# A decoder trunk on one core: who makes the second weight tile's high part in the front, and how many filler matmuls stand there

## The chip, the core and the metric

The kernel runs on one core of a Trainium2 chip. The metric is the device time of one execution in microseconds (us). Five engines run their own instruction queues side by side: TensorE (PE; PEld is its weight load), VectorE (DVE), ScalarE (ACT), GpSimd (POOL) and SyncE (SP), which mostly issues DMAs. Before the change the time is 1191.01 us, the median of three runs (1190.72 to 1191.04).

## What is computed

The reference is a small decoder with two layers, 512 tokens and 1024 columns: layer 0 mixes tokens with forgetting attention, layer 1 with a gated short convolution, and each has a squared-ReLU MLP and a gated embedding. Only the very first product matters here, the value projection of the attention:

```python
def rmsnorm(x, g):
    xf = x.astype(jnp.float32)
    y = xf * lax.rsqrt(jnp.mean(xf * xf, axis=-1, keepdims=True) + RMS_EPS)
    return (y * g.astype(jnp.float32)).astype(x.dtype)
...
hn = rmsnorm(x, g[0])
proj = hn @ w_in
v = proj[..., 2 * D:3 * D]
f_logit = (proj[..., 3 * D:] + b_f)
```

## The kernel before

**High and low parts.** All products are made with float32 data that is split into a high part (rounded to the matmul's input format) and a low part (what the rounding left). A product is three matmuls: high x high, low x high and high x low. For a weight tile `raw` the high part `wh` is a scaled copy, and the low part `wl` is `raw` times the scale minus `wh`. The scale is the gain `g` of the norm, one number per partition.

**The value projection** works on `x` as it came, transposed by the host (`xT`), with the gain folded into the weights; the token's norm is applied to the result. Its columns go in three chunks (`V_CHUNKS`); the first has 272 columns, 256 of values and 16 forget-gate logits. `part(c, ps, t, n, fill)` makes the twelve matmuls of chunk c, token block t (of 4) and half n of the contraction (four weight tiles): four with `wh` and `xh`, four with `wh` and `xl`, four with `wl` and `xh`, line 690. The tile of `x` is the stationary operand, the weight tile is streamed, 272 columns at a time.

**The order around the change** is written out by hand (a manual schedule for all engines). SyncE and ScalarE issue the first DMAs (from line 2320): the first block of `xT`, the weight tiles 0 to 3 and then the next blocks. Weight tile 0 (`in_wg`) carries the gains of three norms in 24 more columns; tile 1 comes over SyncE, tile 2 over ScalarE, tile 3 over SyncE. TensorE first runs seven matmuls on a tile of ones (`work(7)`, line 2335), which nobody reads; I call these fillers. VectorE casts the first block of `xT` to its high part (line 838) and copies the gains to `first_g` (line 841); GpSimd makes that block's low part `xl` (line 842). Then `prepare(4)` gives, tile by tile, ScalarE the high part and VectorE the low part (lines 481 and 483). The first ScalarE copy takes its scale from the raw tile, since `first_g` isn't there yet; the other three take it from `first_g`. The first call of `part` gets `fill = (1, 1, 1)`: behind each of its first three matmuls TensorE runs one 512-column filler. After it, the other three token blocks follow, each with its own split of `xT` (ScalarE high, VectorE low, lines 472 and 473), and so on without fillers.

**Beyond the front** the kernel goes through attention, the MLPs, the convolution and the gated embeddings, with the order of work from a planner; the change touches none of it.

Of the kernel before, what the change touches and what calls it, by code (L numbers as in the profile page):

```python
# [8 lines left out]
F32 = mybir.dt.float32  # L9
F32R = mybir.dt.float32r  # L10
AF = mybir.ActivationFunctionType
ALU = mybir.AluOpType
# [3 lines left out]
P = 128  # L16
D = 1024
S = 512
# [6 lines left out]
NEG = -1e30  # L25
PUT_OFF = 46000
LAG = 2
AHEAD = 2
PAGES = 70
RAWS = 14  # L30
LEAD = 1
V_CHUNKS = ((768, 272), (0, 512), (512, 256))
# [182 lines left out]
def trunk(ctx: ExitStack, tc, x, xT, pT, g, wg, wv, wqk, bf, wo, wci, wcq, cw, wco, wup, wdn, wpp, wpg, out):  # L215
    nc = tc.nc
# [10 lines left out]
    def page(name, dtype=F32):  # L227
        return pages.tile([P, S], dtype, tag="pg", name=name)
# [12 lines left out]
    warm = page("warm", F32R)  # L241
# [4 lines left out]
    first_g = consts.tile([P, 3 * KT], F32, tag="first_g", name="first_g")  # L246
# [4 lines left out]
    loads, order, where, ready, fetched, begun = [], [], {}, {}, [], [0]  # L251
# [61 lines left out]
            ],  # L313
        )

    def widest(key):

        return V_CHUNKS[key[1]][1] if key == ("v", 0, 0) else S

    def fetch(upto, engines=(nc.sync,)):  # L320
        while len(fetched) < min(upto, len(loads)):
            n = len(fetched)
# [5 lines left out]
    def banked(key):  # L328

        return key[0] in ("up", "dn") and key[2] // (1 + (key[0] == "up")) in BANKED  # L330
# [25 lines left out]
    def prepare(upto, lows=None):  # L356
        while begun[0] < min(upto, len(order)):
            n = begun[0]
            begun[0] += 1
            key, at = order[n]  # L360
            for of in (key[:3], key[:2]):
                if of in recipes and banked(key):
                    if of not in fetched_of:
                        at_of = recipes[of][0]
                        fetch(max(at_of.values()) + 1)
                        fetched_of[of] = {u: fetched[m] for u, m in at_of.items()}
                    if isinstance(at, tuple):
                        sum_in_bank(of, key[len(of):])
                elif of in recipes:
                    derive(of)  # L370
            hi, lo = page(f"wh{n}", F32R), page(f"wl{n}", F32R)
            if isinstance(at, tuple):
                raw, w = derived[key] if banked(key) else derived.pop(key), S
                eng = nc.gpsimd if (key[0] == "dn" and key[2] > 0) or key[-1] in ON_POOL else nc.vector
                if banked(key):
                    eng = nc.vector
            else:
                fetch(at + 1)
                raw, eng, w = fetched[at], lows or nc.vector, min(loads[at].shape[-1], widest(key))
                if banked(key) and low_on_pool(key):  # L380
                    eng = nc.gpsimd
                fetched[at] = None
            if key[0] in ("v", "qk"):
                split_gained(hi, lo, raw, w, key[2], eng, key[0] == "qk" or key[1] == 2,
                             raw[:, w : w + 1] if key == ("v", 0, 0) else None)
            else:
                split(hi[:, :w], lo[:, :w], raw[:, :w], eng)
            ready[key] = Pair(hi[:, :w], lo[:, :w])

    def wide(*key, soon=SOON):  # L390

# [80 lines left out]
        nc.scalar.copy(hi, src)  # L472
        return eng.tensor_tensor(out=lo, in0=src, in1=hi.bitcast(F32), op=ALU.subtract)

    def split_gained(hi, lo, src, w, at, eng, paired, first=None):

        parts = [(slice(0, w), at)]
        if paired:
            parts = [(slice(256 * i, 256 * i + 256), 2 * at + i) for i in range(2)]
        for c, k in parts:  # L480
            nc.scalar.mul(hi[:, c], src[:, c], first_g[:, k : k + 1] if first is None else first)
        for c, k in parts:
            eng.scalar_tensor_tensor(
                out=lo[:, c], in0=src[:, c], scalar=first_g[:, k : k + 1],
                in1=hi[:, c].bitcast(F32), op0=ALU.mult, op1=ALU.subtract,
            )
# [139 lines left out]
    def attention(hT, raw_x, b_f, warm, work, by_hand):  # L626
# [59 lines left out]
        def part(c, ps, t, n, fill=()):  # L686

            for p, of in ("hi", "hi"), ("lo", "hi"), ("hi", "lo"):
                for k in range(4 * n, 4 * n + 4):
                    nc.tensor.matmul(  # L690
                        ps[:, : V_CHUNKS[c][1]], getattr(of_x(k, t), p),
                        getattr(ready["v", c, k], of),
                        start=k == 0 and p == of, stop=k == KT - 1 and of == "lo",
                    )
                    if p == of and k < len(fill):
                        work(fill[k])

        def values(t):

# [127 lines left out]
        with tc.manual_schedule(engines={E.PE, E.DVE, E.Activation, E.Pool, E.SP}):  # L827
            work(7)
            banks_v = {(0, t): bank(f"v0_{t}") for t in range(NB)}

            def halves(c, *at):
                for t, n in at:
                    if (c, t) not in banks_v:
                        banks_v[c, t] = bank(f"v{c}_{t}")
                    part(c, banks_v[c, t], t, n, (1, 1, 1) if c == t == n == 0 else ())

            first = turned[0, 0] = Pair(*(page(f"x{s}0_0", F32R) for s in "hl"))
            nc.vector.tensor_copy(first.hi[:, :S], raw_x[0][0][:, :S])
            w = V_CHUNKS[0][1]
            gains = fetched[0][:, w : w + 3 * KT]  # L840
            nc.vector.tensor_copy(first_g, gains)
            nc.gpsimd.tensor_tensor(
                out=first.lo[:, :S], in0=raw_x[0][0][:, :S], in1=first.hi[:, :S].bitcast(F32),
                op=ALU.subtract,
            )
            prepare(4)
            halves(0, (0, 0))
            for t in range(1, NB):
                split_x(t, 0)
                halves(0, (t, 0))  # L850
                if t == 2:
                    prepare(6)
            prepare(KT)
            fetch(2 * KT)
            nc.sync.dma_start(b_f, bf[0:1, :].partition_broadcast(P))
            first_x = [load_x("xc", t) for t in range(NB)]
            fetch(RAWS + KT)
            for t in range(NB):
                split_x(t, 1)
                halves(0, (t, 1))  # L860
            tri, ones = page("tri", F32R), page("ones")
            nc.gpsimd.memset(ones[:, :S], 1.0)
            nc.gpsimd.affine_select(
                out=ones[:, :S], in_=ones[:, :S], compare_op=ALU.is_ge, fill=0.0, base=0,
                pattern=[[1, S]], channel_multiplier=-1,
            )
            nc.vector.tensor_copy(tri[:, :S], ones[:, :S])
            prepare(KT + 4)
            halves(1, (0, 0), (1, 0))
            prepare(2 * KT)  # L870
            fetch(RAWS + 2 * KT)
            halves(1, (0, 1), (1, 1))
            for t in range(NB):
                inverse(t)
            halves(1, (2, 0))
            r_rows = rows()
            halves(1, (2, 1), (3, 0), (3, 1))
            for two in ((0, 1), (2, 3)):
                for t in two:
                    logits(t, banks_v[0, t])  # L880
                for t in two:
                    keep_values(0, t, banks_v[0, t])
                prepare(2 * KT + 4)
            steps = logs()
            first_half = normed_x(0, r_rows)
            next(first_half)
            next(steps)
            next(first_half)
            keep_values(1, 0, banks_v[1, 0])
            next(steps)  # L890
            next(first_half)
            keep_values(1, 1, banks_v[1, 1])
            next(steps)
            fetch(RAWS + 2 * KT + 4)
            for _ in first_half:
                pass
            for t in range(1):
                values(t)
            sums_of_logs(tri)
            bias(0)  # L900
            bias(1)
            keep_values(1, 2, banks_v[1, 2])
            prepare(2 * KT + 6)
            for _ in normed_x(1, r_rows):
                pass
            prepare(2 * KT + 8)
            keep_values(1, 3, banks_v[1, 3])
            for t in range(1, NB):
                values(t)
            for n, _ in enumerate(project(0, 0)):  # L910
                if n == KT - 1:
                    prepare(2 * KT + 12)
        def heads_planned():
# [255 lines left out]
            n_sc, done = 4 * H, 8  # L1169
            for c in range(-8, n_sc + LAG):  # L1170
                share = 2 * (c + 9) if c < n_sc - 16 else (
# [1158 lines left out]
    b_f = consts.tile([P, H], F32, tag="bf", name="b_f")  # L2330
    warm_p = bank("warm_p")

    def work(n):
        for _ in range(n):
            nc.tensor.matmul(warm_p, warm[:, :P], warm[:, :S], start=True, stop=True)

    kept = dram.tile([2, NB, 2, P, S], F32, tag="kept", name="kept")
    hT = turned_x
# [119 lines left out]
```

## Time and profile before

| what | us |
|---|---|
| median of three runs | 1191.01 |
| the profiled execution | 1191.42 |
| its span, first to last instruction | 1189.5 |
| TensorE busy | 1180.9 |
| VectorE busy | 1023.0 |
| ScalarE busy | 871.2 |
| GpSimd busy | 610.4 |

The profile is of one execution. "Busy" counts an engine's instructions; a busy TensorE is not TensorE at its peak, since matmuls are pipelined and their durations overlap. The chain is the work that ended last, followed back step by step to what released it. In a timeline a row has the start, the duration, the engine, the line, the operation, output and inputs and the count of merged instructions; a number in square brackets is idle time of the engine before the row, and what ended it. In the rows on DMA issues the last number is the time from issue to landing. The 0.01 us of the views is their rounding, for landings 0.1.

### The profile page before, as it was taken

How to read it: one execution, taken by the hardware profiler on the slowest of the kernel's cores; microseconds unless marked ns; L12 is line 12 of the kernel's file. 1: busy time of each engine (PE TensorE's matmuls, PEld its weight loads, DVE VectorE, ACT ScalarE, POOL GpSimd, SP SyncE). 2: the span in 40 equal slices, each digit the busy share in tenths (PEclk: the TensorE clock that was granted, in tenths of full speed). 3: DMA queues.
4: the chain of work that ended last, by engine and by line, in shares of the span. 5: the costliest groups of instructions: out<-in, count | busy, mean ns of one | idle time of the engine just before them, and what ended most of it. 6: DMA issues, size and time to landing. Idle time of an engine off the chain costs nothing.

```text
span 1189.5 us, 21339 instructions
## 1 busy us (share of the span) xinstructions
PE 1180.9 (99%) x7220; PEld 1059.2 (89%) x7220; DVE 1023.0 (86%) x1789; ACT 871.2 (73%) x1867; POOL 610.4 (51%) x616
## 2 busy tenths in 40 slices
PE   9999999999999999999999999999999999999997
PEld 8888888898899889989889999989889998999886
DVE  7878988589989999988869999858999999998973
ACT  7688888469887888777756766447978878887751
POOL 3035567148557755776313653025775577559410
PEclk9999999999999999999999999999999999999999
DMA  9376754514233324356413233532332333236401
GB/s 340 112 218 167 210 183 116 195 63 119 80 113 115 112 74 136 106 171 201 143 36 99 67 104 115 188 123 63 116 107 84 121 116 115 84 112 205 142 18 53
DMA packets 86606, 149.96 MB, mean 126 GB/s; under 512 B 10144, under 2 KB 17872, under 8 KB 86496
## 3 DMA queue, kind: packets, MB, share of 16 engines
q1 hardware_dynamic: 85920, 148.04, 40.4%
q8 instruction: 57, 0.93, 0.3%
q10 hardware_dynamic: 576, 0.55, 0.1%
q14 instruction: 53, 0.43, 0.1%
HBM read 137.99 MB, written 6.37 MB: 121 GB/s over the span
## 4 chain that ended last, share of the span: by engine, by line
PE 92%; DVE 5%; issue 1%; ACT 1%; DMA 0%; POOL 0%; POOLq 0%; DVEq 0%
PE dn L465 8%; PE dn L464 8%; PE dn L466 8%; PE v L690 3%; PE qk L464 3%; PE qk L466 2%; PE qk L465 2%; PE pg L466 2%; PE pg L464 2%; PE pg L465 2%; PE ps_o L1104 2%; PE up L465 2%; PE up L466 2%; PE up L464 2%; PE pT L1076 1%; PE up_1c L466 1%
## 5 line engine op out<-in xcount | busy, mean ns | idle before, releaser
L1325 ACT CAST wh<-raw 128x512 fp32r<-128x512 f32 x261 | 157.1, 626 | 0.0
L1225 DVE TENSOR_TENSOR acc<-dn,acc 128x512 f32<-128x512 f32 x184 | 118.6, 679 | 6.4 <-PE dn L466 5.8
L1225 POOL TENSOR_TENSOR wl<-raw,wh 128x512 fp32r<-128x512 f32 x86 | 116.6, 1359 | 6.6 <-ACT wh L1325 6.3
L1225 POOL TENSOR_TENSOR s<-m,d 128x256 f32<-128x256 f32 x22 | 16.5, 752 | 156.7 <-ACT m L1745 137.4
L1325 ACT CAST wh<-dn_T 128x512 fp32r<-128x512 f32 x112 | 65.2, 588 | 28.7 <-DVE dn_T L1225 28.4
L1225 DVE TENSOR_TENSOR wl<-up_S,wb 128x512 fp32r<-128x512 f32 x104 | 68.2, 677 | 13.6 <-ACT wb L1329 11.9
L1325 ACT CAST wh<-up_S 128x512 fp32r<-128x512 f32 x104 | 65.5, 630 | 16.6 <-POOL up_S L1225 15.5
L1225 POOL TENSOR_TENSOR up_S<-raw,raw 128x512 f32<-128x512 f32 x52 | 77.0, 1489 | 0.0
L1225 DVE TENSOR_TENSOR wl<-dn_T,wh 128x512 fp32r<-128x512 f32 x112 | 74.6, 680 | 2.7 <-ACT wh L1325 2.7
L1329 ACT CAST wb<-up_S 128x512 fp32r<-128x512 f32 x104 | 62.1, 598 | 9.0 <-DVE acc L1225 4.5
L1225 DVE TENSOR_TENSOR wl<-raw,wb 128x512 fp32r<-128x512 f32 x100 | 65.7, 676 | 2.5 <-ACT wb L1329 2.5
L1225 DVE TENSOR_TENSOR wl<-raw,wh 128x512 fp32r<-128x512 f32 x75 | 60.9, 829 | 4.2 <-ACT wh L1325 4.1
L1329 ACT CAST wb<-raw 128x512 fp32r<-128x512 f32 x100 | 58.9, 596 | 0.0
L464 PE MATMUL qk<-hTh,wh 128*128 128x512 f32 x128 | 51.0, 398 | 0.0
L464 PE MATMUL pg<-wh,hTh 128*128 128x512 f32 x128 | 50.5, 395 | 0.0
L466 PE MATMUL qk<-hTl,wh 128*128 128x512 f32 x128 | 50.2, 392 | 0.0
L465 PE MATMUL qk<-hTh,wl 128*128 128x512 f32 x128 | 50.2, 392 | 0.0
L466 PE MATMUL pg<-wl,hTh 128*128 128x512 f32 x128 | 49.9, 390 | 0.0
L465 PE MATMUL pg<-wh,hTl 128*128 128x512 f32 x128 | 49.8, 389 | 0.0
L1063 POOL TENSOR_SCALAR prl<-prl,rs 128x512 f32<-128x512 f32 x16 | 25.9, 1617 | 44.0 <-DVE rs L1056 44.0
L465 PE MATMUL dn<-wh,S1l 128*128 128x512 f32 x112 | 43.9, 392 | 0.0
L466 PE MATMUL dn<-wl,S1h 128*128 128x512 f32 x112 | 43.7, 390 | 0.0
(846 smaller groups left out, 4956.1 us busy)
## 6 DMA issues: line engine op xcount, KB each, us to landing
raw<-in_wup SPq DMA_DIRECT2D x128, 256.0 KB, 2.9
raw<-in_wdn SPq DMA_DIRECT2D x128, 256.0 KB, 2.7
raw<-in_wcq SPq DMA_DIRECT2D x36, 256.0 KB, 2.8
raw<-in_wqk SPq DMA_DIRECT2D x32, 256.0 KB, 5.2
raw<-in_wpg SPq DMA_DIRECT2D x32, 256.0 KB, 2.8
g<-in_g SPq DMA_DIRECT2D x18, 256.0 KB, 5.5
raw<-in_wo SPq DMA_DIRECT2D x16, 256.0 KB, 4.4
prl<-neg_c SPq DMA_DIRECT2D x16, 256.0 KB, 4.8
```

The costliest lines, as they stand in the source:

```text
L464: nc.tensor.matmul(ps, a.hi, b.hi, start=start, stop=False)
L465: nc.tensor.matmul(ps, a.lo, b.hi, start=False, stop=False)
L466: nc.tensor.matmul(ps, a.hi, b.lo, start=False, stop=stop)
L690: nc.tensor.matmul(ps[:, : V_CHUNKS[c][1]], getattr(of_x(k, t), p), getattr(ready["v", c, k], of), start=k == 0 and p == of, stop=k == KT ...
L1063: nc.gpsimd.tensor_scalar(out=pr, in0=pr, scalar1=stats_of[h][1][:, u : u + 1], scalar2=None, op0=ALU.mult)
L1076: nc.tensor.transpose(ps[0][:, b * P : (b + 1) * P], probs[h][b][:, j * P : (j + 1) * P], ident)
L1104: nc.tensor.matmul(mixed[h][:, j * P :], v, u[:, j * P : S], start=j == 0 and not (stop or last.get(("u", h))), stop=stop)
L1225: eng.tensor_tensor(out=out, in0=x, in1=y, op=op)
L1325: nc.scalar.copy(ready[key].hi[:, both], src())
L1329: nc.scalar.copy(aside[0].bitcast(F32R), src())
```

## The change

Three things change, all in the first microseconds:

- A new function `prepare_first` replaces `prepare(4)`. It makes the four high parts first, with the second tile's on VectorE (a tensor_scalar multiplication) and the others on ScalarE, and puts the four low parts behind all four highs. All of them take their scale from the gains in raw tile 0.
- The copy of the gains to `first_g` moves behind the second tile's high part on VectorE. Later tiles still read `first_g`.
- The fillers in the first `part` become `FILLS = ((0,), (1, 256), (1,))`: none behind the first matmul, one of 256 columns behind the second, one of 512 behind the third.

```diff
+FILLS = ((0,), (1, 256), (1,))
+FIRST_ON_VECTOR = (1,)
...
+    def prepare_first(gains):
+
+        lows = []
+        for n in range(4):
+            key, at = order[n]
+            begun[0] += 1
+            raw, w, scale = fetched[at], V_CHUNKS[0][1], gains[:, n : n + 1]
+            hi, lo = page(f"wh{n}", F32R), page(f"wl{n}", F32R)
+            if n in FIRST_ON_VECTOR:
+                nc.vector.tensor_scalar(
+                    out=hi[:, :w], in0=raw[:, :w], scalar1=scale, scalar2=None, op0=ALU.mult
+                )
+            else:
+                nc.scalar.mul(hi[:, :w], raw[:, :w], scale)
+            fetched[at] = None
+            ready[key] = Pair(hi[:, :w], lo[:, :w])
+            lows.append((raw, scale, hi, lo, w))
+        nc.vector.tensor_copy(first_g, gains)
+        for raw, scale, hi, lo, w in lows:
+            nc.vector.scalar_tensor_tensor(
+                out=lo[:, :w], in0=raw[:, :w], scalar=scale, in1=hi[:, :w].bitcast(F32),
+                op0=ALU.mult, op1=ALU.subtract,
+            )
...
-                    if p == of and k < len(fill):
-                        work(fill[k])
+                    if fill:
+                        work(*fill.pop(0))
...
-                    part(c, banks_v[c, t], t, n, (1, 1, 1) if c == t == n == 0 else ())
+                    part(c, banks_v[c, t], t, n, fills if c == t == n == 0 else [])
...
-            nc.vector.tensor_copy(first_g, gains)
...
-            prepare(4)
+            prepare_first(gains)
...
-    def work(n):
+    def work(n, columns=S):
         for _ in range(n):
-            nc.tensor.matmul(warm_p, warm[:, :P], warm[:, :S], start=True, stop=True)
+            nc.tensor.matmul(
+                warm_p[:, :columns], warm[:, :P], warm[:, :columns], start=True, stop=True
+            )
```

The rest of the diff takes out what `split_gained` and `prepare` needed for the special case of the first tile.

The first rows of TensorE before, from the seven fillers to the first matmul of the low part of `x` (`wh0` to `wh3` are the high parts of the four weight tiles, `xh0_0` and `xl0_0` the high and low part of the first block of `x`):

```order
L2335 MATMUL warm_p_140<-warm_78 128x512 x7
L690 MATMUL v0_0_156<-wh0_165,xh0_0_160 128x272
L2335 MATMUL warm_p_140<-warm_78 128x512
L690 MATMUL v0_0_156<-wh1_169,xh0_0_160 128x272
L2335 MATMUL warm_p_140<-warm_78 128x512
L690 MATMUL v0_0_156<-wh2_173,xh0_0_160 128x272
L2335 MATMUL warm_p_140<-warm_78 128x512
L690 MATMUL v0_0_156<-wh3_177,xh0_0_160 128x272
L690 MATMUL v0_0_156<-wh0_165,xl0_0_161 128x272
```

The same place of TensorE now:

```order
L2357 MATMUL warm_p_140<-warm_78 128x512 x7
L711 MATMUL v0_0_156<-wh0_164,xh0_0_160 128x272
L711 MATMUL v0_0_156<-wh1_167,xh0_0_160 128x272
L2357 MATMUL warm_p_140<-warm_78 128x256
L711 MATMUL v0_0_156<-wh2_170,xh0_0_160 128x272
L2357 MATMUL warm_p_140<-warm_78 128x512
L711 MATMUL v0_0_156<-wh3_173,xh0_0_160 128x272
L711 MATMUL v0_0_156<-wh0_164,xl0_0_161 128x272
```

The filler between the first two matmuls is gone, and the next one is half as wide.

The first rows of VectorE before (`wl` are the low parts of the weight tiles, `xl1_0` the low part of the second block of `x`):

```order
L838 CAST xh0_0_160<-xT0_0_93 128x512
L841 COPY first_g_86<-raw0_102 128x24
L483 SCALAR_TENSOR_TENSOR wl0_166<-raw0_102,first_g_86,wh0_165 128x272
L483 SCALAR_TENSOR_TENSOR wl1_170<-raw1_104,first_g_86,wh1_169 128x272
L483 SCALAR_TENSOR_TENSOR wl2_174<-raw2_106,first_g_86,wh2_173 128x272
L483 SCALAR_TENSOR_TENSOR wl3_178<-raw3_108,first_g_86,wh3_177 128x272
L473 TENSOR_TENSOR xl1_0_197<-xT1_0_95,xh1_0_196 128x512
```

The same place of VectorE now:

```order
L861 CAST xh0_0_160<-xT0_0_93 128x512
L396 TENSOR_SCALAR wh1_167<-raw1_104,raw0_102 128x272
L404 COPY first_g_86<-raw0_102 128x24
L406 SCALAR_TENSOR_TENSOR wl0_165<-raw0_102,wh0_164 128x272
L406 SCALAR_TENSOR_TENSOR wl1_168<-raw1_104,raw0_102,wh1_167 128x272
L406 SCALAR_TENSOR_TENSOR wl2_171<-raw2_106,raw0_102,wh2_170 128x272
L406 SCALAR_TENSOR_TENSOR wl3_174<-raw3_108,raw0_102,wh3_173 128x272
L494 TENSOR_TENSOR xl1_0_196<-xT1_0_95,xh1_0_195 128x512
```

`wh1` has come in behind the cast, ahead of the copy of the gains; the low parts keep their order, and ScalarE loses `wh1` between `wh0` and `wh2`. GpSimd's and SyncE's rows stay in place, and from the second block of `x` on TensorE's, VectorE's and ScalarE's do too.

More of the change, by code (lines that the diff above doesn't have):

```diff
@@ L314, in plan_sevens @@
         )
-    def widest(key):
-        return V_CHUNKS[key[1]][1] if key == ("v", 0, 0) else S
     def fetch(upto, engines=(nc.sync,)):
@@ L378, in prepare @@
                 fetch(at + 1)
-                raw, eng, w = fetched[at], lows or nc.vector, min(loads[at].shape[-1], widest(key))
+                raw, eng, w = fetched[at], lows or nc.vector, loads[at].shape[-1]
                 if banked(key) and low_on_pool(key):
@@ L383, in prepare @@
             if key[0] in ("v", "qk"):
-                split_gained(hi, lo, raw, w, key[2], eng, key[0] == "qk" or key[1] == 2,
-                             raw[:, w : w + 1] if key == ("v", 0, 0) else None)
+                split_gained(hi, lo, raw, w, key[2], eng, key[0] == "qk" or key[1] == 2)
             else:
@@ L473, in split, with split_gained @@
         return eng.tensor_tensor(out=lo, in0=src, in1=hi.bitcast(F32), op=ALU.subtract)
-    def split_gained(hi, lo, src, w, at, eng, paired, first=None):
+    def split_gained(hi, lo, src, w, at, eng, paired):
         parts = [(slice(0, w), at)]
@@ L480, in split_gained @@
         for c, k in parts:
-            nc.scalar.mul(hi[:, c], src[:, c], first_g[:, k : k + 1] if first is None else first)
+            nc.scalar.mul(hi[:, c], src[:, c], first_g[:, k : k + 1])
         for c, k in parts:
@@ L829, in attention @@
             banks_v = {(0, t): bank(f"v0_{t}") for t in range(NB)}
+            fills = list(FILLS)
             def halves(c, *at):
```

## The prediction

> **What bounds the kernel now.** I read the page's busy time, its chain and TensorE's (PE's) own waits first, to see what a change in the first microseconds can be worth at all.
>
> ```profile
> PE 1180.9 (99%) x7220; PEld 1059.2 (89%) x7220; DVE 1023.0 (86%) x1789; ACT 871.2 (73%) x1867; POOL 610.4 (51%) x616
> PE 92%; DVE 5%; issue 1%; ACT 1%; DMA 0%; POOL 0%; POOLq 0%; DVEq 0%
> PE warm_p L2335 <- POOL warm L242: 1.4, 1, 1.4
> PE up_0a L465 <- DVE wl L1225: 0.3, 2, 0.2
> ```
>
> TensorE is busy for 99% of the span, the chain that ended last runs on it for 92%, and its waits add up to 1.7 us. No DMA has a share of the chain. So a matmul that starts x us earlier in the front brings the end x us nearer, unless something near the front is late. The chain in order of time shows the front.
>
> ```profile
> 0.78 3.42 DMA raw<-in_wg
> ...
> 4.23 0.53 ACT wh L481
> ...
> 4.80 0.60 PE v L690
> ...
> 7.13 23.05 PE v L690 x142
> ```
>
> The first weight tile lands, ScalarE (ACT) makes its high part `wh0`, TensorE starts at 4.80 and never stops again here. The timeline of TensorE in this stretch:
>
> ```profile
> 1.36 3.35 PE L2335 MATMUL warm_p<-warm 128*128 128x512 f32 x7 [1.36 <-POOL warm L242]
> 4.80 0.60 PE L690 MATMUL v<-wh,xh 128*128 128x272 f32 x1
> 5.19 0.63 PE L2335 MATMUL warm_p<-warm 128*128 128x512 f32 x1
> 5.62 0.43 PE L690 MATMUL v<-wh,xh 128*128 128x272 f32 x1
> 5.85 0.63 PE L2335 MATMUL warm_p<-warm 128*128 128x512 f32 x1
> 6.27 0.43 PE L690 MATMUL v<-wh,xh 128*128 128x272 f32 x1
> 6.50 0.63 PE L2335 MATMUL warm_p<-warm 128*128 128x512 f32 x1
> 6.93 0.43 PE L690 MATMUL v<-wh,xh 128*128 128x272 f32 x1
> 7.15 0.84 PE L690 MATMUL v<-wh,xl 128*128 128x272 f32 x4
> 7.38 0.61 PE L690 MATMUL v<-wh,xl 128*128 128x272 f32 x3
> 7.83 0.67 PE L690 MATMUL v<-wl,xh 128*128 128x272 f32 x4
> 8.34 0.66 PE L690 MATMUL v<-wh,xh 128*128 128x272 f32 x4
> ```
>
> Durations overlap, so I go by starts. Up to 7.38 a 272-column matmul takes 0.227 us from start to start (7.15 to 7.38) and a 512-column filler 0.43 (5.19 to 5.62, and likewise the other two). From 7.83 on, four 272-column matmuls take 0.51, or 0.127 each. TensorE's clock nearly doubles between 7.38 and 7.83. In the row of 7.38 the last of three starts at 7.71 (7.38 + 0.61, less the 0.66 - 3 x 0.127 = 0.28 that one takes), so the short spacing begins at about 7.59, and I put the change at 7.55.
>
> **The change part by part.** *TensorE.* The filler after the first matmul goes and the next one is halved: 0.43 + 0.21 = 0.64 us at the slow clock. The new starts, if every operand is there: first matmul up to 5.19, second 5.19, 256-column filler 5.42, third 5.63, filler 5.86, fourth 6.29, the low-part matmuls from 6.51 instead of 7.15. What counts is how far TensorE is when its clock rises. If that stays at 7.55, it is 0.64 / 0.227 = 2.8 matmuls ahead there, and each of these would have taken 0.127 at the fast clock: **a gain of 0.36 us**. If the clock rose 0.64 earlier too, the whole 0.64 would be gained; I take the fixed time, because nothing removed lets TensorE be busy any earlier.
>
> *Operands.* ScalarE, VectorE (DVE) and GpSimd (POOL) in the same stretch, with the issues and landings of the weight tiles:
>
> ```profile
> 4.23 0.52 ACT L481 ACTIVATE wh<-raw 128x272 fp32r<-128x272 f32 x1 [1.03 <-DMA raw<-in_wg]
> 4.66 0.52 ACT L481 ACTIVATE wh<-raw,first_g 128x272 fp32r<-128x272 f32 x1
> 5.57 0.53 ACT L481 ACTIVATE wh<-raw,first_g 128x272 fp32r<-128x272 f32 x1
> 4.03 0.43 DVE L838 CAST xh<-xT 128x512 fp32r<-128x512 f32 x1 [4.03 <-DMA xT<-in_xT]
> 4.37 0.17 DVE L841 COPY first_g<-raw 128x24 f32<-128x24 f32 x1
> 4.54 1.27 POOL L842 TENSOR_TENSOR xl<-xT,xh 128x512 fp32r<-128x512 f32 x1 [2.71 <-DVE first_g L841]
> 4.78 2.92 DVE L483 SCALAR_TENSOR_TENSOR wl<-raw,first_g,wh 128x272 fp32r<-128x272 f32 x4 [0.24 <-ACT wh L481]
> 4.78 1.33 DVE L483 SCALAR_TENSOR_TENSOR wl<-raw,first_g,wh 128x272 fp32r<-128x272 f32 x1 [0.24 <-ACT wh L481]
> 6.03 0.49 DVE L483 SCALAR_TENSOR_TENSOR wl<-raw,first_g,wh 128x272 fp32r<-128x272 f32 x1
> 1.23 0.89 SPq L326 DMA_DIRECT2D raw<-in_wv  x2
> raw<-in_wv ACTq DMA_DIRECT2D x1, 136.0 KB, 3.6
> raw<-in_wv SPq DMA_DIRECT2D x1, 136.0 KB, 3.3
> raw<-in_wv SPq DMA_DIRECT2D x1, 136.0 KB, 3.9
> ```
>
> `wh2` and `wh3` stay on ScalarE. Tile 2, issued beside tile 1 at 1.23, lands at 1.23 + 3.6 = 4.83, so `wh2` is done at 4.83 + 0.52 = 5.35, wanted at 5.63. Tile 3, SyncE's second issue at about 1.7, lands at 5.6; its copy already starts at 5.57 now and ends at 6.10 as before, wanted at 6.29. Taking `wh1` off ScalarE thus gains nothing for `wh3`, and the filler that stays covers that landing. Reading the scales from the raw tile is worth nothing alone: the second ScalarE copy ran 0.43 behind the first, by its own pace.
>
> `wh1` is the one that decides. Its tile lands at 1.23 + 3.3 = 4.53, known to 0.05 because the view rounds. The new VectorE operation is not in this trace; its nearest rows are the same operation on another tile:
>
> ```profile
> L671 DVE TENSOR_SCALAR neg_c<-c_T 16x384 f32<-16x384 f32 x1 | 0.4, 401 | 0.0
> L671 DVE TENSOR_SCALAR neg_c<-c_T 16x256 f32<-16x256 f32 x1 | 0.3, 334 | 0.0
> ```
>
> 272 columns lie 16 above 256: 334 + 16 x 67/128 = 342 ns. Tile 0 landed at 4.20 and was read at 4.23, so the new operation starts 0.03 behind its tile, at 4.56; undisturbed, `wh1` is there at 4.90, 0.29 before TensorE wants it at 5.19. Behind it in VectorE's queue wait the copy of the scales (only the fifth tile's copy, some 3 us later, needs it), the four low parts and the first `xl`. No DMA issue and no GpSimd or SyncE instruction changes place. The low parts are hardly moved: the first now takes 1.33 where an undisturbed one takes 0.49, because it sits behind GpSimd's operation (4.54 to 5.81), and so it would again. They end at 4.78 + 2.92 = 7.70; TensorE would want the fourth at about 7.9. That cover is 0.2 us. Should VectorE's new operation hold GpSimd up instead by some 0.3, the low parts end near 8.0 and TensorE waits about 0.2, which leaves 0.16 of the gain. Between 0.16 and 0.36 I take 0.3, nearer to the unhindered end, because only the last of four low parts would be late.
>
> **The weak point** is that GpSimd's operation starts at 4.54, the same moment at which tile 1 lands. Two pairs elsewhere show what such a meeting does:
>
> ```profile
> 874.00 1.83 POOL L1225 TENSOR_TENSOR up_S<-raw,raw 128x512 f32<-128x512 f32 x1
> 874.01 0.68 DVE L1225 TENSOR_TENSOR S1l<-s,S1h 128x512 fp32r<-128x512 f32 x1
> 969.18 1.29 POOL L1225 TENSOR_TENSOR wl<-raw,wh 128x512 fp32r<-128x512 f32 x1
> 969.23 1.79 DVE L1225 TENSOR_TENSOR dn_T<-raw,raw 128x512 f32<-128x512 f32 x1
> ```
>
> 0.01 us behind GpSimd, VectorE went first and GpSimd took 1.83; 0.05 behind, VectorE took 1.79 where it needs 0.68. Starting between 4.51 and 4.61, the new operation would come 0.03 before to 0.07 behind GpSimd's. But each of these VectorE operations reads two tensors; the new one reads one tensor and a column of scales, and no row here shows such an operation held up. GpSimd's row also names the copy of the scales as what it waited for, though it reads only the cast's output: if that is right, GpSimd now starts behind the new operation and the meeting is off. So I bound `wh1` by 4.90 and by the end of GpSimd's operation, 5.81, plus about 0.17 (272 columns at 67 ns per 128 are 0.14, and some start-up): 5.98. I forecast the first end: on the rows, only two-tensor operations are held.
>
> [...]
>
> **Rivals.** *VectorE is held and the clock rises late (slower).* `wh1` at 5.98 leaves TensorE without work from 5.19 to 6.03, for the filler that stood there is gone. Second matmul 6.03, filler 6.26, third 6.47, filler 6.70, fourth 7.13, low parts from 7.35: 0.20 behind now, or 0.20 / 0.227 x 0.127 = 0.11 at the end. The price is the clock. Before, it rose 7.55 - 4.80 = 2.75 after the unbroken run began, and 7.55 - 1.36 = 6.2 after the first filler. If the hole of 0.84 starts this anew at 6.03, it rises between 8.8 and 12.2, and TensorE runs slow for 1.25 to 4.65 us longer: 5.5 to 20.5 matmuls at 0.100 more, 0.55 to 2.05, with the 0.11 a loss of 0.66 to 2.16. The middle, 1.4, gives 1192.4. It decides once `wh1` comes so late that the hole outweighs what counted as busy before. For it: the race is close, and the pause before (4.71 to 4.80) was small beside this hole. [...]
>
> *VectorE is held, the clock rises on time.* Then only the 0.11 is lost: 1191.1. For it: fillers from 1.36 may count for the clock whatever follows.
>
> *The gain is eaten later, or the change does nothing.* Low parts, `xl1` or a transfer come late and take the rest: 1191.0. Against it: with 0.2 us of cover for the low parts, more would have to go late than the rows show.
>
> **How the numbers follow.** The profiled execution took 1191.42, 1.92 more than its span of 1189.5; the median of the three runs is 1191.01. The forecast is 1191.42 - 0.3 = 1191.1 for an execution with a profile, and 1191.01 - 0.3 = **1190.7** for the median.
> Chances: forecast 0.50, held with a late clock 0.30, held with the clock on time 0.13, eaten or nothing 0.05, anything else 0.02. The range must take in the slower rival, since leaving it out leaves out 3 in 10: from 1190.3 (the whole 0.64 gained, and a little scatter, since the runs span 0.3) to 1193.2 (that rival's far end, 2.16). The forecast's own range is 1190.3 to 1190.9. About 0.2%, or 2.4 us, is what a measurement of this kernel can tell from no change; no priced case reaches it. Faster by that much 0.01; slower 0.04, if the late clock costs more than its far end; the same 0.95.
>
> **What would show it.** Right: the second 272-column matmul starts near 5.2, VectorE's new row takes about 0.34, the low-part matmuls start near 6.5, the short spacing begins near 7.55. Wrong: the new row takes over 1 us and ends with GpSimd's, TensorE has a hole from 5.2 to 6.0; then the start of the short spacing tells the two held cases apart. If TensorE waits at the fourth low part near 7.9, that cover was mis-sized. If all steps hold and the time is still off by more than 0.5, the gain was lost or found far from the front.

## The result: 0.12% slower, and the profile after

The changed kernel takes 1192.6 us, the median of 22 runs (1191.38 to 1193.2), against 1190.8 for the kernel before, also of 22 (1190.49 to 1191.47). The ratio on record is 1.0012, with an interval of 1.0007 to 1.0018 (the two medians alone give 1.0015), so the change is small but clear of noise. I had forecast 0.3 us less; it is 1.8 us more, close to the 1192.4 of the first rival. The 22 runs lie in two groups, 9 from 1191.38 to 1191.92 and 13 from 1192.28 to 1193.2.

The profiled execution took 1192.58, its span is 1190.8 (before: 1191.42 and 1189.5). VectorE and GpSimd in the timeline of the front; L396 is the new operation, the high part of tile 1:

```profile
4.06 0.43 DVE L861 CAST xh<-xT 128x512 fp32r<-128x512 f32 x1 [4.06 <-DMA xT<-in_xT]
4.63 1.82 DVE L396 TENSOR_SCALAR wh<-raw,raw 128x272 fp32r<-128x272 f32 x1
6.45 0.85 DVE L406 SCALAR_TENSOR_TENSOR wl<-raw,wh 128x272 fp32r<-128x272 f32 x1
7.22 1.32 DVE L406 SCALAR_TENSOR_TENSOR wl<-raw,raw,wh 128x272 fp32r<-128x272 f32 x3
4.57 1.26 POOL L864 TENSOR_TENSOR xl<-xT,xh 128x512 fp32r<-128x512 f32 x1 [2.75 <-DVE xh L861]
5.78 0.52 POOL L884 MEMSET ones<- 128x512 f32 x1
6.38 0.63 POOL L885 TENSOR_SCALAR_AFFINE_SELECT ones<-ones 128x512 f32<-128x512 f32 x1
```

GpSimd's subtraction starts at 4.57, VectorE's new operation 0.06 later, and instead of 0.34 it takes 1.82. It ends at 6.45: not just behind the subtraction (5.83), but behind the memset that follows it (6.30). The first low part takes 0.85, where 0.49 is undisturbed, beside GpSimd's select (from 6.38). The four low parts then end at 8.54 instead of 7.70.

The chain shows why VectorE came second. Tile 1 landed when the prediction said, at 1.23 + 3.30 = 4.53, but the operation starts 0.10 behind its tile, not the 0.03 that ScalarE had shown; the 4.56 of the prediction would have been just ahead of GpSimd's 4.57, and whether that wins isn't shown:

```profile
1.23 3.30 DMA raw<-in_wv
...
4.63 1.83 DVE wh L396
```

TensorE:

```profile
4.82 0.60 PE L711 MATMUL v<-wh,xh 128*128 128x272 f32 x1
6.51 0.59 PE L711 MATMUL v<-wh,xh 128*128 128x272 f32 x1 [1.09 <-DVE wh L396]
6.90 0.41 PE L2357 MATMUL warm_p<-warm 128*128 128x256 f32 x1
7.12 0.43 PE L711 MATMUL v<-wh,xh 128*128 128x272 f32 x1
7.34 0.63 PE L2357 MATMUL warm_p<-warm 128*128 128x512 f32 x1
7.77 0.43 PE L711 MATMUL v<-wh,xh 128*128 128x272 f32 x1
8.00 1.11 PE L711 MATMUL v<-wh,xl 128*128 128x272 f32 x4
8.90 1.06 PE L711 MATMUL v<-wl,xh 128*128 128x272 f32 x4
9.80 0.67 PE L711 MATMUL v<-wh,xh 128*128 128x272 f32 x4
10.31 0.66 PE L711 MATMUL v<-wh,xl 128*128 128x272 f32 x4
```

The hole stands from about 5.2, where TensorE could start the next matmul, to 6.51 (the row counts 1.09 of it as idle). The low-part matmuls begin at 8.00 (before 7.15) and stay 0.22 to 0.23 apart (8.90 to 9.80 for four) until the next block begins at 9.80. Before, four took 0.51 from 7.83 on. Read from this spacing, the clock rises about 2.2 us later here, and this execution is 9.80 - 8.34 = 1.46 behind at that point. Near the end, in the chain, the step before the last normalization shows what is left of it, before and after:

```profile
1175.97 0.70 DVE e L2150
```

```profile
1177.26 0.70 DVE e L2172
```

1.29 of the 1.46 reach the end; only 0.17 was made up on the way.

### The profile page after: what moved, and what is told of

It is laid out like the page before. It is cut to its first block, busy times and chain, and to the rows that moved or that the text cites. A ratio compares the mean times of both kernels' runs of the same rounds, so it can differ in the third digit from the quotient of the medians.

```text
span 1190.8 us, 21336 instructions
## 1 busy us (share of the span) xinstructions
PE 1181.1 (99%) x7219; PEld 1059.4 (89%) x7219; DVE 1023.4 (86%) x1790; ACT 870.7 (73%) x1866; POOL 610.3 (51%) x616
## 4 chain that ended last, share of the span: by engine, by line
PE 92%; DVE 5%; issue 1%; ACT 1%; DMA 0%; POOL 0%; POOLq 0%; DVEq 0%; SPq 0%
PE dn L486 8%; PE dn L485 8%; PE dn L487 8%; PE v L711 3%; PE qk L485 3%; PE qk L487 2%; PE qk L486 2%; PE pg L485 2%; PE pg L487 2%; PE pg L486 2%; PE ps_o L1126 2%; PE up L486 2%; PE up L485 2%; PE up L487 2%; PE pT L1098 1%; PE up_1c L487 1%
## 5 line engine op out<-in xcount | busy, mean ns | idle before, releaser
L485 PE MATMUL dn<-wh,S1h 128*128 128x512 f32 x112 | 43.6, 389 | 0.0
```

Source lines behind the costliest of these rows:

```text
L485: nc.tensor.matmul(ps, a.hi, b.hi, start=start, stop=False)
```

## The experiments

All eleven were timed beside the kernel before, 11 runs each; none leaves work of the reference out. With differences near 0.1%, the intervals of all but the last hold 1; so the verdicts rest on the rows, on the groups of runs, and only then on medians. Beside the last three experiments the kernel before stands at 1191.37, some 0.3 higher than beside the others, so only differences carry over.

**All four high parts on ScalarE.** One line of the changed kernel:

```diff
-FIRST_ON_VECTOR = (1,)
+FIRST_ON_VECTOR = ()
```

> All four high parts on ScalarE again (scales from the raw tile, low parts behind the highs, new fillers kept). Theory, the hold: VectorE's high part of tile 1 was held by GpSimd and left TensorE a hole, so without that operation the second matmul starts at 5.2 to 5.3, the low-part matmuls near 6.5, the short spacing about where it was before, and the time is 0.2 to 0.4 below the kernel before: 1190.4 to 1190.6. Rival, too few fillers: 768 columns less keep TensorE's clock low for longer whoever makes the high part: no hole, but the short spacing begins 2 us later and the time stays near 1192. Rival, late low parts: TensorE waits for the low parts behind the four highs, 1191.5 or more, with waits at the wl matmuls.

1190.7 beside 1191.05, ratio 0.9998 (0.999 to 1.0007); ten runs from 1190.55 to 1191.04 and one at 1192.14. The median is a little above the 1190.4 to 1190.6 expected. The slower time is gone with the one VectorE operation, though the fillers are still 768 columns fewer: that rival falls. The profile shows a front in which the clock rose early, and what bounds it then:

```profile
5.00 0.81 PE L711 MATMUL v<-wh,xh 128*128 128x272 f32 x2 [0.40 <-ACT wh L400]
...
6.47 0.67 PE L711 MATMUL v<-wh,xl 128*128 128x272 f32 x4
6.98 1.33 PE L711 MATMUL v<-wl,xh 128*128 128x272 f32 x4
8.15 0.66 PE L711 MATMUL v<-wh,xh 128*128 128x272 f32 x4
```

At the fast clock a row of four matmuls is 0.66 long and the next starts 0.5 behind it; here the four `wl` matmuls take 1.33 and the next block starts 1.17 behind, because VectorE delivers the low parts only that fast (the last ends at 7.87). The rival with the late low parts is right so far: in such a run they are the bound; its price of 1191.5 or more was too high. The kernel before has the same bound when its clock is up early (8.11, in the next experiment), so in such a run this version gains nothing there.

**The hole filled.** `wh1` stays on VectorE and late; three fillers stand where TensorE would idle:

```diff
-FILLS = ((0,), (1, 256), (1,))
+FILLS = ((3,), (0,), (0,))
```

> Tile 1's high part stays on VectorE and stays held; the fillers move: three of 512 columns behind the first matmul, none later, so TensorE has work from 4.8 to 6.5. Theory, the hold with a late clock: the second matmul still starts at 6.5, but the short spacing begins near 7.5 again, since nothing interrupts TensorE; low-part matmuls from 7.2; the low parts of the weights end near 8.5 and cost 0.3 to 0.5; 1190.8 to 1191.4. Rival, the late high part costs by itself and not by the clock: near 1192.5 as the changed kernel.

1191.91 beside 1191.05, ratio 1.0006 (0.9997 to 1.0015). Nine runs lie from 1191.45 to 1192.05, only two above (1192.69 and 1193.03), where the changed kernel had 13 of 22 in the upper group (and 7 of 11 in the last experiment). So the upper group goes with the hole, not with the late `wh1`. But the lower group stays some 0.7 above the kernel before; I had allowed 0.3 to 0.5 at most for the low parts. VectorE and TensorE in its profile:

```profile
7.26 1.31 DVE L406 SCALAR_TENSOR_TENSOR wl<-raw,raw,wh 128x272 fp32r<-128x272 f32 x3
```

```profile
6.54 0.65 PE L711 MATMUL v<-wh,xh 128*128 128x272 f32 x3 [0.33 <-DVE wh L396]
7.53 1.49 PE L711 MATMUL v<-wl,xh 128*128 128x272 f32 x4
8.85 0.66 PE L711 MATMUL v<-wh,xh 128*128 128x272 f32 x4
```

The clock was up before 6.54 here, not near 7.5 as expected, so the three fillers were short (0.94 together) and 0.33 of the hole was left. The last low part ends at 8.57 and TensorE's next block starts only at 8.85. The profile of the kernel before with eight fillers (an experiment below), also with an early clock, has it at 8.11:

```profile
6.92 1.36 PE L690 MATMUL v<-wl,xh 128*128 128x272 f32 x4
8.11 0.67 PE L690 MATMUL v<-wh,xh 128*128 128x272 f32 x4
```

The difference of 0.74 is the second cost of the held operation.

**GpSimd's subtraction on VectorE.** The low part of the first block of `x` is made by VectorE behind `wh1`, so GpSimd has nothing to do there and makes the mask at 1.8.

```diff
-            nc.gpsimd.tensor_tensor(
-                out=first.lo[:, :S], in0=raw_x[0][0][:, :S], in1=first.hi[:, :S].bitcast(F32),
-                op=ALU.subtract,
-            )
-            prepare_first(gains)
+            prepare_first(gains, first, raw_x[0][0])
...
+        nc.vector.tensor_tensor(
+            out=first.lo[:, :S], in0=x0[:, :S], in1=first.hi[:, :S].bitcast(F32), op=ALU.subtract
+        )
         nc.vector.tensor_copy(first_g, gains)
```

> GpSimd's subtraction (low part of the first block of x) goes to VectorE, behind tile 1's high part; the mask then starts on GpSimd at about 1.9, since nothing stands ahead of it. Theory, the hold: the new VectorE operation takes 0.34, high part of tile 1 at 4.9, second matmul at 5.2, low-part matmuls near 6.5; no low part is held, the four end near 7.3; 1190.3 to 1190.6. Rival, VectorE's operation is slow by itself (a one-tensor multiplication with a column of scales from a raw tile): it still takes 1.8 and the time stays near 1192.5. Rival, too few fillers: no hole but a late clock, near 1192.

```profile
4.62 0.36 DVE L396 TENSOR_SCALAR wh<-raw,raw 128x272 fp32r<-128x272 f32 x1 [0.34 <-DMA raw<-in_wv]
4.90 0.68 DVE L404 TENSOR_TENSOR xl<-xT,xh 128x512 fp32r<-128x512 f32 x1
```

The operation takes 0.36 once GpSimd is out of the way; it isn't slow by itself. 1190.93 beside 1191.05, ratio 0.9998 (0.9989 to 1.0006), one run of 11 at 1192.8. That is above the 1190.3 to 1190.6 expected. TensorE in this profile waited 0.2 for the fourth high part, whose tile lands when it lands, whatever the fillers do.

**The mask ahead of the subtraction.** GpSimd's memset and select move in front, so nothing follows the subtraction.

```diff
             first = turned[0, 0] = Pair(*(page(f"x{s}0_0", F32R) for s in "hl"))
+            tri, ones = page("tri", F32R), page("ones")
+            nc.gpsimd.memset(ones[:, :S], 1.0)
+            nc.gpsimd.affine_select(
...
-            tri, ones = page("tri", F32R), page("ones")
-            nc.gpsimd.memset(ones[:, :S], 1.0)
-            nc.gpsimd.affine_select(
```

> The two GpSimd operations that make the mask (a memset and a select) stand ahead of its subtraction, so behind the subtraction GpSimd has nothing. In the changed kernel VectorE's operation ended 0.62 behind the subtraction, just behind the memset. Theory, the memset holds it too: now it ends 0.15 to 0.2 behind the subtraction, near 6.0, the hole shrinks from 1.1 to 0.7; 1191.3 to 1192.4, a little below the changed kernel. Rival, the subtraction alone holds it and the operation needs 0.6 after it: end near 6.45, time as the changed kernel, 1192.5.

```profile
4.77 1.15 DVE L396 TENSOR_SCALAR wh<-raw,raw 128x272 fp32r<-128x272 f32 x1 [0.36 <-DMA raw<-in_wv]
...
6.33 1.31 DVE L406 SCALAR_TENSOR_TENSOR wl<-raw,raw,wh 128x272 fp32r<-128x272 f32 x3
```

```profile
4.50 1.26 POOL L870 TENSOR_TENSOR xl<-xT,xh 128x512 fp32r<-128x512 f32 x1 [1.52 <-DVE xh L867]
```

It ends at 5.92, 0.16 behind the subtraction's 5.76. So the subtraction and the memset each held it in the changed kernel. 1192.26 beside 1191.05, ratio 1.0008 (0.9999 to 1.0017): five runs from 1190.95 to 1191.19, six from 1192.26 to 1193.24. The lower group is back at the time of the kernel before; in its profile (1191.07) the low parts end at 7.64. The upper group stays, as a hole does (0.75 idle in this profile); no profile shows that group.

**GpSimd second.** GpSimd's subtraction waits for VectorE's operation.

```diff
+        ins = nc.gpsimd.tensor_tensor(
+            out=first.lo[:, :S], in0=x0[:, :S], in1=first.hi[:, :S].bitcast(F32), op=ALU.subtract
+        )
+        tc.add_manual_dep(
+            ins.ins, high.ins.name,
+            mybir.DependencyInfo(mybir.DependencyClass.Sync, mybir.DependencyReason.DATA),
+        )
```

> The changed kernel, with one wait more: GpSimd's subtraction starts only when VectorE has made tile 1's high part. Theory, who starts first holds the other: VectorE's operation takes 0.34 to 0.36 and ends near 4.95, the second matmul starts at 5.2, GpSimd's subtraction runs from 5.0 to 6.3 and now holds VectorE's first low part until about 6.6; the fourth low part ends near 8.2, and TensorE waits for it; 1190.8 to 1191.2, without the hole. Rival, the operation is slow whenever GpSimd is busy at all, whoever starts first: it still takes over 1 us, and the time stays near 1192.5.

```profile
5.08 0.36 DVE L396 TENSOR_SCALAR wh<-raw,raw 128x272 fp32r<-128x272 f32 x1 [0.19 <-DMA raw<-in_wv]
5.36 0.17 DVE L411 COPY first_g<-raw 128x24 f32<-128x24 f32 x1
5.44 0.50 DVE L413 SCALAR_TENSOR_TENSOR wl<-raw,wh 128x272 fp32r<-128x272 f32 x1
5.85 2.70 DVE L413 SCALAR_TENSOR_TENSOR wl<-raw,raw,wh 128x272 fp32r<-128x272 f32 x3
5.53 1.55 POOL L404 TENSOR_TENSOR xl<-xT,xh 128x512 fp32r<-128x512 f32 x1 [3.71 <-DVE first_g L411]
```

0.36 again, with GpSimd ordered behind it. The first low part wasn't the one held, as I had thought; it started ahead of GpSimd's subtraction, which took 1.55 instead of 1.26, and the three behind it took 2.70 where 1.3 is undisturbed. They end at 8.55, and the time is 1191.73 beside 1191.02, ratio 1.0007 (0.9999 to 1.0016), seven runs below 1191.9 and four above 1192.5. The hold has moved to the low parts; my 1190.8 to 1191.2 was too low. But that the low parts cost the time isn't shown. In the profiled execution (1191.89) TensorE's rows are

```profile
5.28 0.82 PE L718 MATMUL v<-wh,xh 128*128 128x272 f32 x2 [0.56 <-ACT wh L400]
...
8.20 1.11 PE L718 MATMUL v<-wl,xh 128*128 128x272 f32 x4
9.11 0.73 PE L718 MATMUL v<-wh,xh 128*128 128x272 f32 x4
```

The four `wl` matmuls take 0.91 from start to start, the slow spacing, so there TensorE isn't waiting for the low parts of the weights: its clock rises only near 9.2, without any hole behind the first matmul.

**No fillers.** High parts on ScalarE, nothing between the first matmuls:

```diff
-FILLS = ((0,), (1, 256), (1,))
-FIRST_ON_VECTOR = (1,)
+FILLS = ()
+FIRST_ON_VECTOR = ()
```

> All four high parts on ScalarE and no filler between the first four matmuls, so nothing on TensorE that isn't wanted; no VectorE operation is in the way. Theory, holes delay the clock: the fourth matmul starts near 6.15, 0.1 to 0.2 earlier than with fillers, with idle stretches of 0.2 and 0.3 before it. Where the clock still rises early the time is 1190.4 to 1190.9; in some half of the runs the idle stretches put the rise off and the time is 1191.6 to 1192.6, so the runs fall into two groups. Rival, fillers are only work that delays: all runs are at or below those of the four highs on ScalarE with fillers, 1190.3 to 1190.7.

1191.64 beside 1191.02, ratio 1.0004 (0.9995 to 1.0012): five runs from 1190.53 to 1191.07, six from 1191.64 to 1192.43. No VectorE operation in the way, the operands as in the first experiment, only less work for TensorE, and yet half of the runs are 1 us slower. The rival, fillers as mere delay, falls. Why they are slower is argued, not shown: the profiled execution (1190.95) is of the faster half.

**Eight fillers ahead.** The third experiment's kernel, then the kernel before, with one filler more ahead of the first matmul:

```diff
-            work(7)
+            work(8)
```

> GpSimd's subtraction on VectorE as in the experiment before, and eight fillers instead of seven ahead of the first matmul, which fills TensorE's pause of about 0.4 before it. Theory, busy time decides when the clock rises: fewer slow runs than the 1 in 11 with seven, the rest unchanged; 1190.4 to 1191.0, none above 1191.6. Rival, the eighth filler delays the first matmul whenever the clock is low: 0.1 to 0.2 more than with seven, 1191.0 to 1191.2.

> The kernel before with eight fillers instead of seven ahead of the first matmul, nothing else. Theory, busy time decides when the clock rises: the runs above 1192 that the kernel before shows (5 of 33 beside the last experiments) become rarer, the median moves by less than 0.2: 1190.8 to 1191.1. Rival, those runs have another cause (a late transfer): as many of them as before.

With VectorE's subtraction 1190.69 beside 1191.02, ratio 0.9998 (0.9989 to 1.0007), all runs from 1190.35 to 1191.28. The kernel before with eight: 1190.99, ratio 0.9999 (0.999 to 1.0008), all from 1190.69 to 1191.39. The kernel before itself had runs of 1191.92 and 1192.72 among its 33 here, and 5 of 33 above 1192 beside the first four experiments. None of the 22 runs with eight fillers is there. That fits busy time better than a late transfer, but it isn't shown: beside all experiments the kernel before has 11 of 93 runs above 1191.9, and at that rate 11 runs without one come up about one time in four.

**Both mends at once.** The mask ahead, and two fillers in the smaller hole:

```diff
-FILLS = ((0,), (1, 256), (1,))
+FILLS = ((2,), (0,), (0,))
```

> Both mends at once, the high part of tile 1 still on VectorE and still held by GpSimd's subtraction: the mask stands ahead (that alone left 5 of 11 runs near 1191.1 and 6 above 1192.2), and two fillers of 512 columns stand in the hole (three alone brought all but 2 of 11 below 1192.1, but left them near 1191.7). Theory, two separate costs, the low parts that end late and the clock that rises late: both go, 1190.7 to 1191.2 with at most 1 or 2 of 11 runs above 1192. Rival, one cost with two signs: one group of runs stays above 1191.6 as with either mend alone.

1191.47 beside 1191.37, ratio 1.0002 (0.9993 to 1.0011); nine runs from 1191.18 to 1191.71, two at 1192.93. VectorE's operation is still held:

```profile
4.94 1.12 DVE L396 TENSOR_SCALAR wh<-raw,raw 128x272 fp32r<-128x272 f32 x1 [0.40 <-DMA raw<-in_wv]
```

Yet the median is 0.1 from the kernel before, and neither the group 0.7 higher nor the larger upper group is left. So there are two costs, one for each mend.

**The best version again.** The kernel of the seventh experiment, unchanged.

> GpSimd's subtraction on VectorE and eight fillers, once more, as the version that may beat both kernels: 1190.4 to 1191.0, 0.2 to 0.4 below the kernel before, no run above 1191.6. Rival, its first median was luck: within 0.1 of the kernel before, with a run or more above 1192.

1191.12 beside 1191.37, ratio 0.9997 (0.9988 to 1.0006), all runs from 1191.03 to 1191.28, while 4 of the 27 of the kernel before were at 1192.3 or above. Twice the median is 0.25 to 0.33 lower and no run falls out; by its intervals it isn't shown to be faster.

**The changed kernel again,** unchanged.

> The changed kernel as it is, for its two groups of runs and a second profile. Theory: again a group near 1191.6 and a larger one near 1192.7. If the profile falls into the first, TensorE's short spacing begins before the hole, near 5, and TensorE waits for the low parts of the weights, which end near 8.5; if into the second, the short spacing begins after 8.8. Rival, the groups have nothing to do with the clock: a profile near 1191.6 with a late clock, or near 1192.7 with an early one.

1193.31 beside 1191.37, ratio 1.0011 (1.0002 to 1.002); four runs from 1191.64 to 1192.13, seven from 1193.03 up. The profiled execution took 1193.42 and shows the clock as such. The granted clock of a stretch reads 1.00 in the first profile even where the spacing is still slow (8.00 to 9.80), so up to its first change I go by the spacing. Each row is a stretch, its length, the busy times of TensorE, its weight loads, VectorE, ScalarE and GpSimd, and the granted clock; the last two columns are DMA:

```profile
4.90:8.10 3.20, 1.66 (x10) 1.41 (x11) 3.15 (x5) 2.40 (x5) 2.36 (x3) 1.00 1.02 355
8.30:11.50 3.20, 3.20 (x15) 3.04 (x14) 3.20 (x8) 2.89 (x6) 0.00 (x0) 0.50 1.01 298
11.70:15.00 3.30, 3.30 (x29) 3.30 (x28) 3.30 (x8) 3.07 (x5) 0.00 (x0) 1.00 1.00 370
```

```profile
8.00:8.19 0.19, 0.19 (x4) 0.19 (x3) 0.19 (x2) 0.00 (x0) 0.00 (x0) 1.00 0.94 225
8.21:8.40 0.19, 0.19 (x3) 0.19 (x2) 0.19 (x2) 0.15 (x1) 0.00 (x0) 0.50 0.79 234
11.40:11.60 0.20, 0.20 (x3) 0.20 (x3) 0.20 (x2) 0.00 (x0) 0.00 (x0) 0.50 1.19 389
11.62:11.80 0.18, 0.18 (x3) 0.18 (x3) 0.18 (x1) 0.00 (x0) 0.00 (x0) 1.00 0.99 364
```

TensorE's rows in the same execution:

```profile
5.18 0.39 PE L711 MATMUL v<-wh,xh 128*128 128x272 f32 x1 [0.46 <-ACT wh L400]
6.83 0.39 PE L711 MATMUL v<-wh,xh 128*128 128x272 f32 x1 [1.26 <-DVE wh L396]
...
7.66 0.67 PE L711 MATMUL v<-wh,xl 128*128 128x272 f32 x4
8.17 1.34 PE L711 MATMUL v<-wl,xh 128*128 128x272 f32 x4
9.31 1.11 PE L711 MATMUL v<-wh,xh 128*128 128x272 f32 x4
10.22 1.11 PE L711 MATMUL v<-wh,xl 128*128 128x272 f32 x4
...
11.85 0.66 PE L711 MATMUL v<-wh,xh 128*128 128x272 f32 x4
```

The block of the last row, in the profile of the kernel before:

```profile
9.84 0.66 PE L690 MATMUL v<-wh,xh 128*128 128x272 f32 x4
```

My expectation was that an execution of the upper group has a late rise. This one had an early rise, which is the sign that I had given to the rival (an upper time with an early clock), and lost it: the four matmuls from 7.66 take 0.51, then at 8.20 the clock is halved, four matmuls take 0.91 (9.31 to 10.22), and only at 11.61 is it back. So the clock does bear on the time of this execution, but by a fall, not by a late rise. The block at 11.85 starts 2.01 later than in the kernel before, and the whole execution is 2.00 longer (1193.42 against 1191.42); some 0.35 of it was there from the start, since VectorE could read the first block of `x` at 4.38 and not at 4.03. That the hole brought the fall about is my guess, since TensorE was busy for only 1.66 of the 3.20 us ahead of it; no run shows the cause.

## Why the prediction was wrong

- **The step that failed** is "I forecast the first end: on the rows, only two-tensor operations are held." VectorE's multiplication of one tensor by a column of scales is held by GpSimd as well: 1.82 in the changed kernel, 1.15 with only the subtraction behind it, 0.36 with GpSimd out of the way or started second. That was inferred from the lack of a row, and a lack of rows bounds nothing. Of the two races that the rows did show, the one 0.05 us behind and held was the better measure for a start 0.06 behind.
- **The start was taken from another engine.** "Tile 0 landed at 4.20 and was read at 4.23, so the new operation starts 0.03 behind its tile" is ScalarE's row; on VectorE it was 0.10 (4.53 to 4.63). That alone doesn't decide: in three other profiles the tile landed later, and the operation came 0.27 to 0.38 behind GpSimd's. The hope that GpSimd waits for the copy of the scales failed as well: its row now names the cast, and it starts 0.08 behind the cast's end in both profiles (4.46 to 4.54, 4.49 to 4.57).
- **The far end was mis-sized too.** The end of GpSimd's operation "plus about 0.17" is what the mask experiment shows (5.92, or 0.16 behind). In the changed kernel it was 6.45, since I hadn't looked at what GpSimd does next: the memset starts at 5.78, before VectorE gets in. The hole was 1.3, not 0.84.
- **The first rival's mechanism was right in the main.** In both profiles of the changed kernel a slow clock stands behind the hole (up to 9.80 in one, from 8.20 to 11.61 in the other), and with the hole filled the upper group shrinks from 13 of 22 to 2 of 11. Its price of 1.4 (forecast 1192.4, measured 1192.6) fitted partly by luck. I took one path for every run, but the clock rises at different moments from run to run: the profiles of the two executions of the changed kernel have it once before and once after the hole (the first matmul takes 0.39 in the one and 0.60 in the other). Two groups fit that, but it isn't shown: both profiles are of the upper group. The lower-group profiles of the hole-filled and the mask kernels do have an early clock; that of the kernel with GpSimd second (1191.89) has a late one.
- **The low parts were judged to be covered** by 0.2 us. With `wh1` held they end 0.84 later (8.54 against 7.70), and where the clock is up early that alone costs about 0.7 (8.85 against 8.11 in the rows of the filled hole). The lower group of the changed kernel fits the same cost, without a profile of it. In the profiled execution the low parts cost nothing: TensorE, at the slow clock, wanted the first at 8.90. The rival had no term for them.
- **The gain of 0.36** assumed a clock that rises at 7.55, as in the one profile that I had. The four timings with fillers and without a held operation show 0.35, 0.12, 0.33 and 0.25 less than the kernel before beside them, none beyond its interval. Where the clock is up early, a 512-column filler costs 0.24 (7.30 to 7.54 in the second profile of the changed kernel) and not 0.43, and the profiles show tile 3's landing (0.2) and the low parts (8.15 against 8.11) as bounds.
- **Operands, part by part,** went mostly as worked out: 0.36 undisturbed against 342 ns for the new operation, ScalarE's `wh2` in time, no other queue in the way. `wh3` was in time only because the hole covered it; with GpSimd's subtraction on VectorE TensorE waited 0.2 for it.
- **The least change that can be told** was put at 0.2%; the 22 runs told 0.12%.
- **How far the hold and the clock are shown.** The 0.36, 1.15 and 1.82 above show the hold where GpSimd is first. The other way round the runs don't show it for `tensor_scalar`: where that was first, the program made GpSimd wait for it. There GpSimd's subtraction took 1.55 instead of 1.26, behind a low part, which reads two tensors. The granted clock was 0.50 from 8.20 to 11.61, 3.41 us, behind a stretch in which TensorE was busy for 1.66 of 3.20; one profile shows this fall, and none shows what brings the fall or the return.

What stays open: whether it is TensorE's busy time that decides when the clock rises or falls, why the moment of the rise differs from run to run, what sets the two groups, and whether the best version's 0.3 us is real.

## What to carry to other kernels

Before an operation is given to an idle VectorE, look at what GpSimd runs at that moment and right behind it: here GpSimd started first, and VectorE waited for two of its instructions in a row; the third, 0.08 behind, held only a later VectorE operation, the first low part (0.85 instead of 0.49). Take the start of a new operation from rows of its own engine. A filler matmul was worth its time here where it closed a hole; take one out only when the operand behind it is sure to come, and time such a change over many runs, since one profile shows one moment of the clock's rise. Where an operation gets late, follow what is queued behind it too: here the late low parts alone cost about 0.7 us where the clock was up early.

## What the runs showed of the hardware

- A GpSimd memset, which reads nothing, held VectorE's one-tensor multiplication: it ended 0.62 behind the subtraction with the memset there, 0.16 without.
- VectorE's operation started 0.10 behind the landing of its tile (4.53 to 4.63), ScalarE's 0.03 (4.20 to 4.23).
- VectorE, waiting since 4.63, did not get in between two GpSimd instructions that followed each other without a pause (4.57 to 5.83 and 5.78 to 6.30); it ended at 6.45.
- TensorE's granted clock, once up, went from 1.00 to 0.50 at 8.20 in one profile, behind a stretch in which it was busy for 1.66 of 3.20 us, and took 3.41 us to return.
